# Mixture-of-experts stage: gate and up weights in one ring slot and one 512-column product per quadrant

## The chip, the cores and the metric

The kernel runs on one core of a Trainium2 chip. The metric is device time in microseconds (us); the kernel before takes 1612.64 us, the median of three runs (1609.98 to 1615.09).

## The reference, cut to what matters

Two layers of a hybrid attention network on 256 latent and 256 context tokens of width 1024, in float32. The last part, about half of the time, is the mixture of experts of layer 1: each of the 256 latent tokens goes to two of eight SwiGLU experts.

```python
for e in range(N_EXPERTS):          # 8 experts, D = 1024, FF = 2816
    out = out + combine[..., e:e + 1] * (silu(h @ wg[e]) * (h @ wu[e])) @ wd[e]
```

Every expert has three float32 matrices of 1024 x 2816; together they are 8 x 3 x 11.5 MB = 276.8 MB, and each byte is read from HBM once.

## The kernel before

**Tokens.** For each expert, `gather` (L966) picks the tokens that chose it into `gh`, up to 96 columns: three groups of 32. The third group holds tokens only where an expert was chosen by more than 64 of them. Products for the third group stand in a branch (`third`, L1011) that TensorE takes or skips by a register; the code of a skipped branch still lies in the program. In this input experts 1, 5, 6 and 7 take it, experts 0, 2, 3 and 4 skip it (experts are counted from 0).

**Columns.** FF is cut into three column groups `GR` (L910): 1024, 1024 and 768 columns. A product is cut over the four column quadrants of the array: `quads` (L1003) issues four products, each of 32 stationary columns and 256 (third group of columns: 192) moving columns, to PSUM partitions 0, 32, 64 and 96. I call these four products a set. Each product has 128 rows of the contraction behind it, one row block k; D has eight (KT = 8).

**One step** is one expert and one column group. `gate` (L1026) runs `half` (L1014): for each of eight row blocks, a set for token group 0 and one for group 1, then the branch with eight sets for group 2 into the bank `gu2`. Silu goes to ScalarE (L1034). `up` (L1037) does the same with the up matrix, into a second PSUM bank; the bank tag "mm" has two buffers. Between `gate` and `up` stand the transposes of the step before (`turn`), pieces of the output (`spread`), and the gathers of the next experts. After `up` comes `down` (L1073) of the step before: eight row blocks (six in the third column group), two sets each, and again a branch. So one step has three branches, and the eight experts have 72.

**Weights.** They pass through a ring of 14 slots of 8 KB per partition (1 MB; `ring`, L932 and L950). `load` (L935) fills one slot with one transfer of two row blocks of one matrix; `plan` (L921) lists them: four gate slots, four up slots, then four (three) down slots of the step before. `fetch` (L957) issues the load for a slot that comes free and hands out the oldest loaded one. All loads go through the queue of SyncE (SP), in order. A slot is free again once all its products are done, those in the branch too, so four slots are held until a branch is passed. The first four slots are loaded before the routing, while layer 1's mixer still runs.

After the last step come the last `turn`, `down`, `collect` and `spread`, and the output is stored.

Of the kernel before, what the change touches and what calls it, by code (L numbers as in the profile page):

```python
# [10 lines left out]
AF = mybir.ActivationFunctionType  # L11
# [4 lines left out]
D = 1024  # L16
KT = 8
# [5 lines left out]
NE = 8  # L23
# [3 lines left out]
LAT, CTX = (0, 1), (2, 3)  # L27
# [14 lines left out]
def build(tc, x, c, ctx, c_ctx, w_ada, b_ada, norm_mix, norm_ffn, w_in, w_out, a_q_gain, a_k_gain,  # L42
# [4 lines left out]
    dma = nc.sync.dma_start  # L47
    act, dve, pool, pe = nc.scalar, nc.vector, nc.gpsimd, nc.tensor
# [6 lines left out]
    def bank(tag, dt=F32):  # L55
        return psp.tile([128, 512], dt, name=tag, tag=tag, bufs=PB[tag])
# [24 lines left out]
    X = [Xl[:, 0], Xl[:, 1], Xc[:, 0], Xc[:, 1]]  # L81
# [28 lines left out]
    p = bank("tp")  # L110
# [4 lines left out]
    p = bank("tp")  # L115
# [44 lines left out]
    def krows(w, k0, kn, c0, cn):  # L160
        return w.rearrange("(k p) n -> p k n", p=128)[:, k0:k0 + kn, c0:c0 + cn]

    pin = tc.keep_in_program_order
# [739 lines left out]
    def moe(l):  # L903
# [6 lines left out]
        GR = ((0, 256), (1024, 256), (2048, 192))  # L910
        mark = [None, None, None]

        def up_rows(w, e, g):
            c0, n = GR[g]
            return [krows(w[m, e], 2 * j, 2, c0, 4 * n) for j in range(4)]

        def down_rows(wd, g):
            c0, n = GR[g]
            return [krows(wd, c0 // 128 + 2 * j, 2, 0, D) for j in range(n // 64)]

        def plan():  # L921
            prev = None
            for e in range(NE):
                for g in range(3):
                    for w in (moe_w_gate, moe_w_up):
                        yield from up_rows(w, e, g)
                    if prev:
                        yield from down_rows(moe_w_down[m, prev[0]], prev[1])
                    prev = e, g
            yield from down_rows(moe_w_down[m, prev[0]], prev[1])  # L930
# [1 line left out]
        ring = [(wa, f"wr{i}") for i in range(NRA)]  # L932
        count = [0]

        def load(src):  # L935
            p, t = ring[count[0] % len(ring)]
            count[0] += 1
            r = p.tile([128, 2048], F32, name="w", tag=t)
            a, b = src.shape[1:]
            v = r[:, 0:a * b].rearrange("p (a b) -> p a b", a=a)  # L940
            dma(v, src)
            return v

        todo = plan()
# [55 lines left out]
            act.copy(q, pt[0:CAP, 0:256].bitcast(F32))  # L1000
            return q

        def quads(ps, c0, lhsT, rhs, n, start, stop):  # L1003
            for q in range(4):
                o, r = ps[32 * q:32 * q + 32, c0:c0 + n], rhs[:, q * n:q * n + n]
                if n == 192:
                    o = o.rearrange("p (c i) -> p c i", c=3)
                    r = rhs.rearrange("p (c q i) -> p q c i", c=3, q=4)[:, q]
                pin(pe.matmul(o, lhsT, r, start=start, stop=stop, tile_position=(0, 32 * q), skip_group_check=True))  # L1009

        def third(m):  # L1011
            return tc.If(m > 0) if m is not None else ExitStack()

        def half(gh, n, pa, o, w, m):  # L1014
            vs = []
            for j in range(4):
                vs.append(w())
                for kk in range(2):
                    k = 2 * j + kk
                    for t in range(2):  # L1020
                        quads(pa, t * n, gh[:, k, 32 * t:32 * t + 32], vs[j][:, kk], n, k == 0 and t == 0, k == KT - 1)
            with third(m):
                for k in range(KT):
                    quads(gu2, o, gh[:, k, 64:96], vs[k // 2][:, k % 2], n, k == 0, k == KT - 1)

        def gate(gh, g, w, m=None):  # L1026
            n = GR[g][1]
            s = bank("mm"), bank("mm")
            sg = mp.tile([128, 832], F32, name="msg", tag="msg", bufs=2)
            if n == 192:  # L1030
                pool.memset(sg[:, 0:64], 0.0)
            s = *s, sg[:, 64:64 + 3 * n], sg
            half(gh, n, s[0], 0, w, m)
            act.activation(s[2][:, 0:2 * n], s[0][:, 0:2 * n], AF.Silu)  # L1034
            return s

        def up(gh, g, s, w, m=None):  # L1037
            n = GR[g][1]
            gA, uA, sg, full = s
            act.activation(sg[:, 2 * n:3 * n], gu2[:, 0:n], AF.Silu)  # L1040
            half(gh, n, uA, 256, w, m)
            dve.tensor_mul(sg[:, 0:2 * n], sg[:, 0:2 * n], uA[:, 0:2 * n])
            dve.tensor_mul(sg[:, 2 * n:3 * n], sg[:, 2 * n:3 * n], gu2[:, 256:256 + n])  # L1043
            return full

        def turn(sg, g):
            n = GR[g][1]
# [25 lines left out]
        def down(aT, g, py, w, m=None):  # L1073
            vs = []
            for i, ts in enumerate(aT):
                if i % 2 == 0:
                    vs.append(w())
                for t in range(2):
                    quads(py[0], 256 * t, ts[t], vs[-1][:, i % 2], 256, g == 0 and i == 0 and t == 0,
                          g == 2 and i == len(aT) - 1)  # L1080
            with third(m):
                for i, ts in enumerate(aT):
                    quads(py[1], 0, ts[2], vs[i // 2][:, i % 2], 256, g == 0 and i == 0, g == 2 and i == len(aT) - 1)

        def collect(py):
            ysb = mp.tile([CAP, D], F32, name="ysb", tag="ysb", bufs=1)
# [35 lines left out]
        def gathers(es_):  # L1122
            perm, gh = gather([col(posm, e) for e in es_], iota)
            for i, e in enumerate(es_):
                where[e] = perm, i, gh[:, i]
# [5 lines left out]
        more = [(big >> e) & 1 for e in range(NE)]  # L1131
        gathers((0, 1))
        units = []
        pend = None
        for e in range(NE):
            gh = where[e][2]
            for g in range(3):
                s = gate(gh, g, fetch, more[e])
                if pend:
                    aT = turn(pend[0], pend[1])  # L1140
                for _ in range(2):
                    if units:
                        spread(*units.pop(0))
                if g == 0:
                    py = [bank("at"), y2] if e == 0 else py
                if e % 2 == 1 and e < NE - 1 and g == 0:
                    gathers((e + 1, e + 2))
                if (e, g) == (NE - 2, 0):
                    gate_rows(l, 1, gm, (0,))
                if e == NE - 1 and g == 2:  # L1150
                    for t in LAT:
                        dve.tensor_mul(acc[:, t], acc[:, t], gm[:, 0])
                        dve.tensor_add(acc[:, t], acc[:, t], X[t])
                if g == 1:
                    qT = permT(where[e][0], where[e][1])
                sg = up(gh, g, s, fetch, more[e])
                if pend:
                    down(aT, pend[1], py, fetch, more[e - (pend[1] == 2)])
                    if pend[1] == 2:
                        ys = collect(py)  # L1160
                        units += [(qT, col(comb, e - 1), ys, t, dh, "tp", e == 1) for dh in range(2) for t in LAT]
                        py = [bank("at"), y2]
                pend = sg, g
# [7 lines left out]
        for rnd in range(1, (NL + CAP - 1) // CAP):  # L1171
            with tc.If(over > CAP * rnd):
                io = mp.tile([128, CAP], F32, name="io", tag="io")
                dve.tensor_scalar(io, iota, float(CAP * rnd), None, op0=OP.add)
                with tc.For_i(0, NE, 1) as e:
                    pc = mp.tile([128, 2, 2], F32, name="pc", tag="pc", bufs=1)
                    dve.tensor_copy(pc[:, :, 0:1], posm[:, :, bass.ds(e, 1)])
                    dve.tensor_copy(pc[:, :, 1:2], comb[:, :, bass.ds(e, 1)])
                    perm, gh = gather([[pc[:, t, 0:1] for t in LAT]] * 2, io)
                    qT = permT(perm, 0)  # L1180

                    def src(w):
                        return w[m, bass.ds(e, 1)].rearrange("o r n -> (o r) n")

                    def rows(parts):
                        it = iter(parts)
                        return lambda: load(next(it))

                    py = [bank("at"), y2]
                    for g in range(3):  # L1190
                        c0, n = GR[g]
                        ch = lambda w: [krows(src(w), 2 * j, 2, c0, 4 * n) for j in range(4)]
                        s = gate(gh[:, 0], g, rows(ch(moe_w_gate)))
                        sg = up(gh[:, 0], g, s, rows(ch(moe_w_up)))
                        down(turn(sg, g), g, py, rows(down_rows(src(moe_w_down), g)))
                    ys = collect(py)
                    for dh in range(2):
                        for t in LAT:
                            spread(qT, [pc[:, t, 1:2] for t in LAT], ys, t, dh, "tp", False, True)
# [120 lines left out]
```

## Time and profile before

| | |
|---|---|
| median of 3 runs | 1612.64 us |
| the profiled execution | 1617.77 us |
| its span, first to last instruction | 1616.0 us |
| TensorE busy over the span | 1508.8 us, 93% |
| weight loads busy (beside the products) | 1140.3 us, 71% |
| VectorE, ScalarE, GpSimd busy | 696.5, 482.3 and 2.9 us |
| mean transfer rate over the span | 245 GB/s |
| mean granted TensorE clock | 0.976 |

The profiled execution is 5.1 us above the median, and 1.8 us of it lie outside its span. Products are pipelined and their ends are modelled, so a busy TensorE need not be one at its peak. "issue" is idle time in which the engine waited for nothing that the profile shows. Instructions come through a transfer queue of their own, q8, in pieces of 16 KB; weights come through q1. Each semaphore step of a transfer is a packet under 512 B, 16 for each transfer.

### The profile page before, as it was taken

The numbers are of one execution on the slowest core, as the hardware profiler recorded it, in microseconds if no ns is written. First come the engines' busy times: TensorE is split into PE (matmuls) and PEld (weight loads), VectorE is DVE, ScalarE is ACT, GpSimd is POOL, SyncE is SP. The second block draws the span as 40 slices with busy tenths as digits, with TensorE's granted clock in tenths as the row PEclk, the third lists the DMA queues.
The fourth block names the chain that finished last, engine by engine and source line by source line (L and its number), as shares of the span: only waits on it lengthen the run. The fifth ranks groups of instructions, "written<-read, shape, count | busy, mean of one in ns | idle before, by whom it ended". The sixth has DMA issues, their size and how long they took to land. (4 is left out here: it accounts for less than half of the span.)

```text
span 1616.0 us, 38981 instructions
## 1 busy us (share of the span) xinstructions
PE 1508.8 (93%) x17126; PEld 1140.3 (71%) x17126; DVE 696.5 (43%) x1646; ACT 482.3 (30%) x1043; POOL 2.9 (0%) x17
## 2 busy tenths in 40 slices
PE   8999999999999999999997899998988899999996
PEld 6987767886998889788776566655564566656663
DVE  4797745797387744578954012020201011010122
ACT  3576663633223322267752011010201011110101
POOL 0000000000000000000000000000000000000000
PEclk9999999999999999999998999999999899999997
DMA  9443324265257733234328999999999998989970
GB/s 323 133 131 106 106 79 131 81 202 186 79 171 239 250 96 100 84 92 131 118 89 326 413 416 357 397 409 412 414 408 415 395 361 333 415 304 395 403 275 30
DMA packets 172148, 396.18 MB, mean 245 GB/s; under 512 B 10768, under 2 KB 89516, under 8 KB 171952
## 3 DMA queue, kind: packets, MB, share of 16 engines
q1 hardware_dynamic: 171952, 393.29, 65.9%
q8 instruction: 157, 2.57, 0.6%
q14 instruction: 39, 0.32, 0.1%
HBM read 392.21 MB, written 1.05 MB: 243 GB/s over the span
## 5 line engine op out<-in xcount | busy, mean ns | idle before, releaser
L1009 PE MATMUL mm<-w,gh 128*32 128x256 f32 (+1 forms) x6144 | 338.2, 367 | 27.1 <-issue 15.1
L1009 PEld LDWEIGHTS mm<-w,gh 128*32 128x32 f32 x6144 | 211.9, 111 | 138.3 <-issue 34.0
L1009 PE MATMUL at<-w,aT 128*32 128x256 f32 x3520 | 209.6, 387 | 13.4 <-issue 8.9
L148 ACT CAST w<-w 128x512 fp32r<-128x512 f32 (+1 forms) x244 | 138.5, 605 | 205.1 <-PE mm L167 87.2
L1009 PEld LDWEIGHTS at<-w,aT 128*32 128x32 f32 x3520 | 127.7, 112 | 89.3 <-issue 19.2
L153 DVE TENSOR_TENSOR w<-w 128x1024 fp32r<-128x1024 f32 (+1 forms) x122 | 144.8, 1186 | 98.8 <-ACT w L148 98.5
L1040 ACT ACTIVATE msg<-av 128x256 f32<-128x256 f32 (+1 forms) x24 | 8.8, 367 | 427.7 <-PE av L1009 239.4
L166 PE MATMUL mm<-w,hTh 128*128 128x256 f32 (+1 forms) x360 | 106.9, 298 | 3.2 <-ACT hTh L361 2.9
L167 PE MATMUL mm<-w,hTl 128*128 128x256 f32 (+1 forms) x360 | 106.7, 297 | 0.0
L168 PE MATMUL mm<-w,hTh 128*128 128x256 f32 (+1 forms) x360 | 106.4, 296 | 0.2 <-DVE w L153 0.2
L166 PE MATMUL mm<-w,aTh 128*128 128x256 f32 (+1 forms) x336 | 97.8, 291 | 0.0
L167 PE MATMUL mm<-w,aTl 128*128 128x256 f32 (+1 forms) x336 | 97.1, 289 | 0.0
L168 PE MATMUL mm<-w,aTh 128*128 128x256 f32 (+1 forms) x336 | 96.9, 289 | 0.0
L1054 DVE COPY aT<-tp 128x256 f32<-128x256 f32 x16 | 6.8, 425 | 182.5 <-PE tp L1053 182.5
L1009 PE MATMUL av<-w,gh 128*32 128x256 f32 (+1 forms) x1536 | 81.4, 361 | 0.0
L166 PEld LDWEIGHTS mm<-w,hTh 128*128 128x128 f32 x360 | 68.9, 192 | 7.8 <-ACT hTh L361 3.7
L167 PEld LDWEIGHTS mm<-w,hTl 128*128 128x128 f32 x360 | 69.0, 192 | 4.2 <-issue 2.0
L168 PEld LDWEIGHTS mm<-w,hTh 128*128 128x128 f32 x360 | 69.0, 192 | 4.0 <-issue 2.0
L166 PE MATMUL at<-hTh,w 128*128 128x512 f32 (+1 forms) x192 | 71.3, 373 | 0.3 <-ACT hTh L361 0.3
L167 PE MATMUL at<-hTh,w 128*128 128x512 f32 (+1 forms) x192 | 71.0, 371 | 0.0
L168 PE MATMUL at<-hTl,w 128*128 128x512 f32 (+1 forms) x192 | 70.9, 374 | 0.0
L1043 DVE TENSOR_TENSOR msg<-msg,av 128x256 f32<-128x256 f32 (+1 forms) x24 | 9.6, 398 | 140.7 <-PE av L1009 78.3
(373 smaller groups left out, 2556.0 us busy)
## 6 DMA issues: line engine op xcount, KB each, us to landing
w<-in_moe_w_down SPq DMA_DIRECT2D x88, 1024.0 KB, 10.6
w<-in_moe_w_gate SPq DMA_DIRECT2D x64, 1024.0 KB, 12.5
w<-in_moe_w_up SPq DMA_DIRECT2D x64, 1024.0 KB, 11.7
araw<-in_w_ada SPq DMA_DIRECT2D x80, 512.0 KB, 4.3
w<-in_moe_w_gate SPq DMA_DIRECT2D x32, 768.0 KB, 11.1
w<-in_moe_w_up SPq DMA_DIRECT2D x32, 768.0 KB, 7.8
w<-in_w_in SPq DMA_DIRECT2D x36, 512.0 KB, 3.7
w<-in_dense_w_gate SPq DMA_DIRECT2D x22, 512.0 KB, 5.0
```

The source lines that it names most:

```text
L148: act.copy(h[:, sl], r[:, sl])
L153: dve.tensor_sub(lo[:, sl], r[:, sl], h[:, sl].bitcast(F32))
L166: pe.matmul(ps, ah, bh, start=start, stop=False, skip_group_check=shared)
L167: pe.matmul(ps, al, bh, start=False, stop=False, skip_group_check=shared)
L168: return pe.matmul(ps, ah, bl, start=False, stop=stop, skip_group_check=shared)
L1009: pin(pe.matmul(o, lhsT, r, start=start, stop=stop, tile_position=(0, 32 * q), skip_group_check=True))
L1040: act.activation(sg[:, 2 * n:3 * n], gu2[:, 0:n], AF.Silu)
L1043: dve.tensor_mul(sg[:, 2 * n:3 * n], sg[:, 2 * n:3 * n], gu2[:, 256:256 + n])
L1054: (dve.tensor_copy if c0 else act.copy)(aT[:, c0:c1], pt[:, 0:c1 - c0])
```

## The change

The gate and the up rows of one row block share a ring slot: each slot is filled by two transfers of half a slot, one of either matrix. A product then takes both halves of the slot as its moving operand, 2 x 256 = 512 columns (2 x 192 = 384 in the third column group), and its result fills a PSUM bank with gate beside up. Token groups 0 and 1 have a bank each (the two "mm" buffers), group 2 has `gu2`. `gate` and `up` become `gate_up`: four row blocks for groups 0 and 1, a branch with four sets for group 2, the work that stood between `gate` and `up` (now handed in as `mid`), four more row blocks and a second branch. Then Silu and the multiply run once for each token group. The number of branches per step stays at three. `down`, its slots and its transfers stay as they were.

```diff
-        def up_rows(w, e, g):
+        def up_rows(wg, wu, g):
             c0, n = GR[g]
-            return [krows(w[m, e], 2 * j, 2, c0, 4 * n) for j in range(4)]
+            return [[krows(w, k, 1, c0, 4 * n) for w in (wg, wu)] for k in range(KT)]
...
-        def load(src):
+        def load(parts):
             p, t = ring[count[0] % len(ring)]
             count[0] += 1
             r = p.tile([128, 2048], F32, name="w", tag=t)
-            a, b = src.shape[1:]
-            v = r[:, 0:a * b].rearrange("p (a b) -> p a b", a=a)
-            dma(v, src)
+            v = r[:, 0:2 * parts[0].shape[2]].rearrange("p (a b) -> p a b", a=2)
+            n = 2 // len(parts)
+            for i, src in enumerate(parts):
+                dma(v[:, i * n:i * n + n], src)
             return v
...
+        def pairs(ps, lhsT, v, n, start, stop):
+            if n == 256:
+                o = lambda q: ps[32 * q:32 * q + 32].rearrange("p (u i) -> p u i", u=2)
+                r = lambda q: v[:, :, q * n:q * n + n]
+            else:
+                o = lambda q: ps[32 * q:32 * q + 32, 0:2 * n].rearrange("p (u c i) -> p u c i", u=2, c=3)
+                r = lambda q: v.rearrange("p u (c q i) -> p q u c i", c=3, q=4)[:, q]
+            quads(o, lhsT, r, start, stop)
...
+        def gate_up(gh, g, w, m, mid):
             n = GR[g][1]
-            s = bank("mm"), bank("mm")
+            ps = bank("mm"), bank("mm"), gu2
...
+            for k0 in (0, 4):
+                vs = [w() for _ in range(4)]
+                for k, v in enumerate(vs, k0):
+                    for t in range(2):
+                        pairs(ps[t], gh[:, k, 32 * t:32 * t + 32], v, n, k == 0, k == KT - 1)
+                with third(m):
+                    for k, v in enumerate(vs, k0):
+                        pairs(gu2, gh[:, k, 64:96], v, n, k == 0, k == KT - 1)
+                if k0 == 0:
+                    mid()
+            for t in range(3):
+                a = sg[:, 64 + t * n:64 + t * n + n]
+                act.activation(a, ps[t][:, 0:n], AF.Silu)
+                dve.tensor_mul(a, a, ps[t][:, n:2 * n])
+            return sg
```

## Rows read from the trace of the kernel before

**Rows 1.** The page: TensorE (busy tenths) and the transfer rate, 40 slices.
```profile
PE   8999999999999999999997899998988899999996
GB/s 323 133 131 106 106 79 131 81 202 186 79 171 239 250 96 100 84 92 131 118 89 326 413 416 357 397 409 412 414 408 415 395 361 333 415 304 395 403 275 30
```
**Rows 2.** Windows: each engine's busy us (instructions), granted clock, share of transfer engines, GB/s.
```profile
980.00:1000.00 20.00, 19.17 (x326) 12.99 (x318) 5.60 (x13) 4.61 (x10) 0.15 (x1) 1.00 0.98 392
1000.00:1020.00 20.00, 20.00 (x396) 12.67 (x392) 1.11 (x2) 0.00 (x0) 0.00 (x0) 1.00 0.81 298
1127.00:1212.00 85.00, 73.72 (x1196) 49.94 (x1192) 14.28 (x31) 10.71 (x24) 0.15 (x1) 0.98 1.02 411
1280.00:1301.00 21.00, 17.34 (x261) 10.90 (x264) 2.83 (x5) 0.20 (x1) 0.00 (x0) 0.83 1.00 390
1301.00:1597.00 296.00, 289.54 (x5282) 186.27 (x5274) 43.61 (x82) 30.86 (x71) 0.45 (x3) 1.00 0.84 329
```
**Rows 3.** Groups by line, 1301 to 1597: third-group products of the gate and up matrices.
```profile
L1009 PE MATMUL av<-w,gh 128*32 128x256 f32 (+1 forms) x1152 | 60.8, 361 | 0.0
```
**Rows 4.** Source L941 (the loads), issues of 1266 to 1273, with times to landing.
```profile
L941 SPq DMA_DIRECT2D w<-in_moe_w_gate x4: 368/394/421, 1266.1 to 1273.0; - x4
DMA to landing us min/median/max: 12.9/14.3/15.8
```
**Rows 5.** Timeline of TensorE from 1300: start, us, instructions; expert 5's first products.
```profile
1299.37 2.01 PE L1009 MATMUL at<-w,aT 128*32 128x256 f32 x16
1301.08 6.15 PE L1009 MATMUL mm<-w,gh 128*32 128x256 f32 x96
```
**Rows 6.** Waits of TensorE, 1045 to 1301: in total, times, longest.
```profile
PE mm L1009 <- issue: 11.5, 8, 3.0
PE mm L1009 <- PEq L1022: 7.0, 12, 2.7
PE mm L1009 <- DMA w<-in_moe_w_gate: 1.8, 2, 1.7
```
**Rows 7.** Timeline of TensorE, 1095 to 1102: a stall inside one run of products.
```profile
1094.72 2.02 PE L1009 MATMUL at<-w,aT 128*32 128x256 f32 x18
1099.46 1.71 PE L1009 MATMUL at<-w,aT 128*32 128x256 f32 x27 [2.73 <-issue]
```
**Rows 8.** Transfer queues: instruction pieces in 1097:1099, 1045:1301 and 1303:1587, in this order.
```profile
q8 instruction: 1, 0.02, 2.1%
q8 instruction: 41, 0.67, 1.0%
q8 instruction: 41, 0.67, 0.9%
```
**Rows 9.** Timeline of TensorE in expert 5, back to back: start, us, line, instructions.
```profile
1358.79 10.54 PE L1009 MATMUL at<-w,aT 128*32 128x256 f32 x192
1369.15 4.08 PE L1009 MATMUL mm<-w,gh 128*32 128x192 f32 x96
1373.05 2.78 PE L1009 MATMUL av<-w,gh 128*32 128x192 f32 x64
```
**Rows 10.** Windows with 768 KB (904, 1164) and with 1 MB transfers (920, 1182).
```profile
904.00:918.00 14.00, 12.41 (x182) 6.99 (x186) 1.51 (x3) 0.37 (x1) 0.15 (x1) 0.88 1.03 414
920.00:948.00 28.00, 22.74 (x410) 16.72 (x404) 1.33 (x3) 1.41 (x3) 0.00 (x0) 0.94 1.02 415
1164.00:1178.00 14.00, 12.99 (x204) 8.15 (x208) 3.65 (x9) 1.52 (x3) 0.15 (x1) 1.00 1.00 390
1182.00:1196.00 14.00, 9.56 (x178) 7.53 (x180) 1.83 (x3) 1.41 (x3) 0.00 (x0) 1.00 1.03 414
```
**Rows 11.** Source L203: issues of the 512 KB transfers of another stage, duration in ns.
```profile
L203 SPq DMA_DIRECT2D araw<-in_w_ada x48: 327/328/497, 240.4 to 561.5; - x48
```
**Rows 12.** Groups by line and form, 860 to 1616: Silu and multiply of the third group.
```profile
L1040 ACT ACTIVATE msg<-av 128x256 f32<-128x256 f32 x16 | 6.2, 384 | 235.2 <-PE av L1009 131.3 <-PEq L1022 103.9
L1043 DVE TENSOR_TENSOR msg<-msg,av 128x256 f32<-128x256 f32 x16 | 6.7, 421 | 103.5 <-PE av L1009 59.7 <-PEq L1022 43.8
```

More of the change, by code (lines that the diff above doesn't have):

```diff
@@ L911, in moe @@
         mark = [None, None, None]
-        def up_rows(w, e, g):
+        def up_rows(wg, wu, g):
             c0, n = GR[g]
-            return [krows(w[m, e], 2 * j, 2, c0, 4 * n) for j in range(4)]
+            return [[krows(w, k, 1, c0, 4 * n) for w in (wg, wu)] for k in range(KT)]
         def down_rows(wd, g):
             c0, n = GR[g]
-            return [krows(wd, c0 // 128 + 2 * j, 2, 0, D) for j in range(n // 64)]
+            return [[krows(wd, c0 // 128 + 2 * j, 2, 0, D)] for j in range(n // 64)]
         def plan():
@@ L924, in plan @@
                 for g in range(3):
-                    for w in (moe_w_gate, moe_w_up):
-                        yield from up_rows(w, e, g)
+                    yield from up_rows(moe_w_gate[m, e], moe_w_up[m, e], g)
                     if prev:
@@ L1001, in permT, with quads, rows256 @@
             return q
-        def quads(ps, c0, lhsT, rhs, n, start, stop):
+        def quads(ps, lhsT, rhs, start, stop):
             for q in range(4):
[L1005 to L1009, printed above, removed]
+                pin(pe.matmul(ps(q), lhsT, rhs(q), start=start, stop=stop, tile_position=(0, 32 * q), skip_group_check=True))
+        def pairs(ps, lhsT, v, n, start, stop):
[6 more added lines that the diff above has]
+            quads(o, lhsT, r, start, stop)
+        def rows256(ps, c0, lhsT, v, start, stop):
+            quads(lambda q: ps[32 * q:32 * q + 32, c0:c0 + 256], lhsT, lambda q: v[:, q * 256:q * 256 + 256], start, stop)
         def third(m):
             return tc.If(m > 0) if m is not None else ExitStack()
[L1014 to L1026, printed above, removed]
+        def gate_up(gh, g, w, m, mid):
             n = GR[g][1]
-            s = bank("mm"), bank("mm")
+            ps = bank("mm"), bank("mm"), gu2
             sg = mp.tile([128, 832], F32, name="msg", tag="msg", bufs=2)
@@ L1031, in gate @@
                 pool.memset(sg[:, 0:64], 0.0)
[L1032 to L1044, printed above, removed]
+            for k0 in (0, 4):
[13 more added lines that the diff above has]
+            return sg
         def turn(sg, g):
@@ L1078, in down @@
                 for t in range(2):
-                    quads(py[0], 256 * t, ts[t], vs[-1][:, i % 2], 256, g == 0 and i == 0 and t == 0,
-                          g == 2 and i == len(aT) - 1)
+                    rows256(py[0], 256 * t, ts[t], vs[-1][:, i % 2], g == 0 and i == 0 and t == 0,
+                            g == 2 and i == len(aT) - 1)
             with third(m):
                 for i, ts in enumerate(aT):
-                    quads(py[1], 0, ts[2], vs[i // 2][:, i % 2], 256, g == 0 and i == 0, g == 2 and i == len(aT) - 1)
+                    rows256(py[1], 0, ts[2], vs[i // 2][:, i % 2], g == 0 and i == 0, g == 2 and i == len(aT) - 1)
         def collect(py):
@@ L1133, in moe @@
         units = []
-        pend = None
+        pend = aT = py = qT = None
         for e in range(NE):
@@ L1137, in moe, with mid @@
             for g in range(3):
[L1138 to L1156, printed above, removed]
+                def mid(e=e, g=g):
+                    nonlocal aT, py, qT
+                    if pend:
+                        aT = turn(pend[0], pend[1])
+                    for _ in range(2):
+                        if units:
+                            spread(*units.pop(0))
+                    if g == 0:
+                        py = [bank("at"), y2] if e == 0 else py
+                    if e % 2 == 1 and e < NE - 1 and g == 0:
+                        gathers((e + 1, e + 2))
+                    if (e, g) == (NE - 2, 0):
+                        gate_rows(l, 1, gm, (0,))
+                    if e == NE - 1 and g == 2:
+                        for t in LAT:
+                            dve.tensor_mul(acc[:, t], acc[:, t], gm[:, 0])
+                            dve.tensor_add(acc[:, t], acc[:, t], X[t])
+                    if g == 1:
+                        qT = permT(where[e][0], where[e][1])
+                sg = gate_up(gh, g, fetch, more[e], mid)
                 if pend:
@@ L1190, in moe @@
                     for g in range(3):
[L1191 to L1194, printed above, removed]
+                        sg = gate_up(gh[:, 0], g, rows(up_rows(src(moe_w_gate), src(moe_w_up), g)), None, lambda: None)
                         down(turn(sg, g), g, py, rows(down_rows(src(moe_w_down), g)))
```

## The prediction

> **What bounds the kernel now.** The change touches the expert stage alone, so I read the page's slices first, to see where that stage lies: from about slice 22 (870 us) to the end TensorE is busy throughout and the transfer rate is near or at 415 GB/s [rows 1]. Both look full, so the next view is the windows, cut at the experts. They show two stretches [rows 2]. From 1301 to 1597, experts 5 to 7, TensorE is busy for 289.5 of 296 us at full clock and the transfers run at 329 GB/s: TensorE sets the pace. These are experts with a third token group (1152 records of its products, 384 for each of three experts) [rows 3]. Before 1301, with experts 2 to 4, transfers run at 411 GB/s with a share of 1.02, and TensorE is busy for only 73.7 of 85 us, at clock 0.98: there the transfers look like the limit, with TensorE waiting for weights.
>
> The third view says that it does not wait for weights. Expert 5's first gate slot is issued at 1266.1 and transfers of that time land 12.9 to 15.8 us after issue, median 14.3 [rows 4], so at about 1280.4; TensorE takes it up at 1301.1 [rows 5]. Weights lie ready for 20 us before use. And the idle time before 1301 is put down to "issue" (11.5 us for the "mm" products) and to the sequencer at the branch line (7.0), to gate transfers only 1.8 [rows 6].
>
> What then holds TensorE up? The fourth view, its timeline, has stalls inside a run of products, 2.73 us in one of them, where no branch and no new slot begins [rows 7]; one 16 KB piece of instructions arrives in just these microseconds [rows 8]. Pieces are counted: 41 from 1045 to 1301, one per 6.2 us. My estimate of the code from the source: a set is 16 instructions (four products, each with two weight loads and two records), a wide step 72 sets with its branches, 1152 instructions, a narrow one 66, 1056; an expert is 2 x 1152 + 1056 = 3360, and some 150 for transposes, gathers and spreads (2388 executed in 85 us [rows 2], less 140 sets or 2240). 3510 x 3 / 41 = 257 instructions per piece, so the code of skipped branches is fetched too. Experts 5 to 7 take 41 pieces as well, over 284 us [rows 8]. So before 1301 TensorE is fed instructions at one piece per 6.2 us while transfers are saturated: 13.7 pieces or 85 us per expert, though the executed sets need 108 x 0.432 + 32 x 0.325 = 57 us [rows 9], some 62 with transposes and gathers (my estimate). It happens that 85 us is also nearly what the transfers need: 34.6 MB at 414 GB/s [rows 10] are 83.6 us. Hence a full ring beside full transfers.
>
> A rule of the Trainium skill, "Runtime: NRT & Kernel Launch", section "Instruction fetch mechanics", says that pieces of 256 instructions are fetched ahead, sequentially and mostly hidden, and that a taken branch with its target outside the fetched window stalls. The first half fits 256 and not "hidden" (2.73 us in mid-run); by the second half alone the stalls would stay, since the branches stay at 72. That is rival B.
>
> **The change, part by part.**
>
> *Products.* Back to back, 24 sets of 256 columns take 1358.79 to 1369.15, 431.7 ns each; 12 of 192 take 1369.15 to 1373.05, 325.0 [rows 9]. That is 1.667 ns per column and 5 ns fixed. A set of 512 replaces two of 256: 858.5 against 863.4 ns. The same columns pass; only the 5 ns go, 480 times in the stage, 216 times after 1301: 1.1 us. No row shows quadrants with 512 columns; the bounds are 0 and 2 us gain, since 192 to 256 is linear. I take 1.
>
> *Instructions.* The gate and up sets halve: a wide step has 2 x (128 + 64) + 384 = 768 instructions, a narrow one 672, an expert 2208 + 150 = 2358, 9.2 pieces, at 6.2 us 57 us. For experts 0, 2, 3, 4 this falls below their products (62) and the transfers (84). TensorE then runs ahead until the ring is empty, and what is late next is the weights. While it was two near-equal limits, one is left, the transfers; expert 5 starts when its first slot lands and no longer 20.7 us later (1301.1 - 1280.4). This is the term that carries the forecast.
>
> *Transfers recovered.* During expert 1 (third group, TensorE slow) the ring was full and transfers idled: 392 and 298 GB/s in two windows of 20 us [rows 2], against 414: 20 x (1 - 392/414) + 20 x (1 - 298/414) = 6.7 us. With the ring nearly empty when expert 1 starts, there is room, and all later landings come up to 6.7 us earlier. I take 6.
>
> *Half transfers.* 116 more transfers pass before expert 5 (24 slots for each of five experts, less four loaded earlier). SP issues one in 0.33 us [rows 11], two per 2.5 us of slot transfer, so its queue is not the limit; "free slot" is waited for once per slot as before, and down's loads stand behind it as before. For a fixed cost per transfer I compare 768 KB with 1 MB: 414 against 415 GB/s with a deep queue (1.900 and 2.527 us; a line through both has 0.02 us at zero bytes), 390 against 414 at 1164 (2.016 and 2.533; 0.465 us) [rows 10]. So 2 to 54 us, never a gain. I take 2: after the change the queue is deep, as in the first pair, and in the second the ring was full and SP waited for slots.
>
> *Expert 5 from an empty ring.* Its first four slots land 2.5 us apart, 7.5 us in all, and the last slot's products follow (two sets, 1.7 us): 9.2 instead of 6.9. Loss 2.3, and after that its products are slower than the transfers. *Clock.* After stalls the clock falls to half; the window before expert 5 has 0.83 over 21 us, 3.6 us lost [rows 2]. Waits for weights could do the same: 0 to 4, I take 2.
>
> *One PSUM bank per token group.* The next step's first product now waits for Silu and multiply of the same bank, 384 and 421 ns [rows 12], three pairs in a row about 1.7 us. `down`'s 7.8 us or more on TensorE hides it. Only between the first and second step there is no `down`; about 1 us once, absorbed by expert 0's surplus. ScalarE and VectorE do one instruction more per step; both are nearly idle. Branches, `mid` and `down` have the same place in the order; two semaphores per slot instead of one on TensorE's sequencer run ahead of the products: 0.
>
> Sum: 20.7 + 6 + 1 - 2 - 2.3 - 2 = 21.4 us. The profiled execution, 1617.8 with 1.8 outside its span, comes to 1596.4; taken from the median, 1612.6 - 21.4 = 1591.
>
> **The rivals.**
>
> *A, smaller (the lead is only partly released).* Expert 0 to 4 still stall on some pieces: in `down`, 384 instructions per 7 us of executed products exceed one piece per 6.2 us, and the clock falls there. If half of the 20.7 us stays, 1601. For it: `down` is not made denser. Against: on average over a step there is slack of 84 to 57.
>
> *B, no change.* The stalls belong to taken branches, 72 as before, and each costs the same: expert 5 starts where it did, 1 us of column gain, 1611. For it: 7.0 us stand at the branch line [rows 6]. Against: the stall in mid-run [rows 7] and pieces in proportion to all code [rows 8].
>
> *C, slower.* Half transfers have a fixed cost that shows when the ring is always waiting for them. At 0.465 us it is 54 us up to expert 5: 1591 + 52 = 1643. It decides from (21.4 + 2) / 116 = 0.20 us per transfer. For it: the second pair of [rows 10]. Against: the first pair, and the share of 1.02 at 411 GB/s, which leaves no idle time between transfers of 1 MB. The Trainium skill, "DMA: Bandwidth & Descriptors", section "Anatomy of one DMA — SWDGE (gpsimd) path", gives a fit of about 2 us per transfer plus bytes at 436 GB/s; were that not overlapped, 116 x 2 = 232 us would be added. The rows disagree at 1 MB, 2.53 us a transfer and not 4.4.
>
> **How the numbers follow.** A measurement can tell 0.3%, 4.8 us, from no change. Forecast 0.66, 1591, its own range 1580 to 1600; A 0.13, 1601; B 0.13, 1611; C 0.08, up to 1643. The range reaches down to 1579 (no clock loss, no first-slot loss, full recovery, and 5 us for the spread of the median) and up to 1607, which takes in A and leaves out B and C, 0.21. Faster: forecast and A, 0.79; same: B, 0.13; slower: C, 0.08.
>
> **What would show it.** Instruction pieces per skipping expert fall from 13.7 to about 9; TensorE's waits before expert 5 change from "issue" to transfers; expert 5 starts near 1280 and lasts with 6 and 7 for about 295 us still; weights lie ready for a few us at most before expert 5. Wrong it is if TensorE's waits stay "issue" at the same cadence (B), if the rate before expert 5 falls under 400 GB/s (C), or if products of 512 columns take over 870 ns a set.

## The result and the profile after

The kernel after takes 1585.74 us (median of four runs, 1584.25 to 1589.97), the one before 1611.31 in the four runs beside them: 0.9851 of the time, interval 0.9829 to 0.9872, so 25.6 us or 1.5% less. The forecast was 1591 us with a range of 1579 to 1607. The profiled execution of after took 1584.25 us, its span is 1582.5 us. The medians leave out one slow run, 1698.70 us at a mean granted clock of 0.84, the fourth run of the changed kernel with another order of experts.

First the slices of the page, as in [rows 1]: the granted clock, in tenths, and the rate.

```profile
PEclk9999999999999999999998999999999999999997
GB/s 322 144 133 108 108 67 134 69 200 224 69 169 213 261 135 87 107 64 132 126 41 280 415 416 415 415 416 403 417 407 416 405 416 406 417 373 399 399 242 30
```

From slice 23 to 35 the rate stays between 403 and 417 GB/s, where [rows 1] have dips to 357, 361 and 333. The clock has its one dip in slice 22, ahead of the experts, and then holds until the last slice.

Next the windows as in [rows 2], with the same columns: expert 1, experts 3 and 4, and experts 5 to 7 of after.

```profile
930.00:1026.00 96.00, 94.07 (x1131) 45.39 (x1127) 14.84 (x34) 11.23 (x27) 0.15 (x1) 1.00 1.03 416
1096.00:1180.00 84.00, 72.17 (x809) 31.21 (x802) 14.84 (x34) 11.23 (x27) 0.15 (x1) 1.00 1.02 412
1180.00:1265.00 85.00, 69.92 (x775) 26.91 (x770) 12.22 (x26) 9.19 (x23) 0.15 (x1) 1.00 1.02 411
1265.00:1561.00 296.00, 288.03 (x3550) 128.01 (x3550) 45.02 (x92) 32.43 (x80) 0.45 (x3) 1.00 0.90 356
```

Expert 3 takes 84 us in after and 85 in [rows 2], with nearly the same busy time of TensorE (72.2 and 73.7 us) and the same rate. By that view alone nothing has changed. What TensorE waits for has changed. Its waits from 1026 to 1265 (experts 2 to 4; in total, times, longest), beside [rows 6]:

```profile
PE mm L1005 <- DMA w<-in_moe_w_up: 11.5, 22, 0.8
PE at L1005 <- DMA w<-in_moe_w_down: 8.8, 15, 1.5
PE mm L1005 <- PEq L1033: 2.7, 8, 0.4
```

The 11.5 us of "issue" are gone, the branch line went from 7.0 to 2.7 us, and 20.3 us in short waits for transfers have come. Instruction pieces of the same stretch, as in [rows 8]:

```profile
q8 instruction: 27, 0.44, 0.7%
```

That is 27 pieces for three experts, 9.0 each, and not 13.7. Expert 5 starts at its first landed slot (timeline of TensorE, as [rows 5]; in brackets the idle time before and what ended it):

```profile
1259.89 1.93 PE L1005 MATMUL at<-w,aT 128*32 128x256 f32 x32 [0.61 <-DMA w<-in_moe_w_down]
1262.74 1.93 PE L1005 MATMUL at<-w,aT 128*32 128x256 f32 x32 [0.92 <-PEq L1079]
1265.01 1.92 PE L1005 MATMUL mm<-w,gh 128*32 128x512 f32 x16 [0.33 <-DMA w<-in_moe_w_up]
1268.02 1.92 PE L1005 MATMUL mm<-w,gh 128*32 128x512 f32 x16 [1.08 <-DMA w<-in_moe_w_up]
1270.31 1.92 PE L1005 MATMUL mm<-w,gh 128*32 128x512 f32 x16 [0.37 <-DMA w<-in_moe_w_up]
```

Where the time went. The stage of the experts begins with the first gather product, and so do the two timelines below, before first, then after:

```profile
869.93 0.50 PE L982 MATMUL tp<-perm,xnh 128*128 128x192 f32 x1 [2.31 <-DVE perm L972]
```

```profile
863.87 0.50 PE L982 MATMUL tp<-perm,xnh 128*128 128x192 f32 x1 [2.31 <-DVE perm L972]
```

The 6.1 us between them lie ahead of the change, in code that is the same in both; the kernels run below, none of which touches that code either, begin their stage between 865 and 868 us, so this is a spread from run to run, and I count from the stage's start:

| us | before | after | gain |
|---|---|---|---|
| stage start to expert 5 | 431.2 (1301.1 - 869.9) | 401.1 (1265.0 - 863.9) | 30.1 |
| experts 5 to 7, to the last product of a weight | 295.8 (to 1596.9) | 295.9 (to 1560.9) | -0.1 |
| from there to the end of the span | 19.1 | 21.6 | -2.5 |
| the stage | 746.1 | 718.6 | 27.5 |

Everything was gained before expert 5. The stage's 27.5 us stand beside 25.6 us between the medians.

### The profile page after: what moved, and what is told of

Read it like the earlier page. It is cut to its first block, busy times and chain, and to the rows that moved or that the text cites. A ratio compares the mean times of both kernels' runs of the same rounds, so it can differ in the third digit from the quotient of the medians.

```text
span 1582.5 us, 31693 instructions
## 1 busy us (share of the span) xinstructions
PE 1486.6 (94%) x13286; PEld 994.2 (63%) x13286; DVE 700.1 (44%) x1670; ACT 486.1 (31%) x1067; POOL 2.9 (0%) x17
## 5 line engine op out<-in xcount | busy, mean ns | idle before, releaser
L1005 PE MATMUL mm<-w,gh 128*32 128x512 f32 (+1 forms) x3072 | 327.5, 559 | 18.0 <-DMA w<-in_moe_w_up 13.3
L1005 PEld LDWEIGHTS mm<-w,gh 128*32 128x32 f32 x3072 | 102.8, 110 | 210.8 <-issue 185.1
L1005 PE MATMUL at<-w,aT 128*32 128x256 f32 x3520 | 202.4, 380 | 12.7 <-DMA w<-in_moe_w_down 8.8
L1005 PEld LDWEIGHTS at<-w,aT 128*32 128x32 f32 x3520 | 118.9, 110 | 100.3 <-DMA w<-in_moe_w_down 19.4
L1005 PE MATMUL av<-w,gh 128*32 128x512 f32 (+1 forms) x768 | 81.1, 557 | 0.0
L1068 DVE COPY aT<-tp 64x256 f32<-64x256 f32 x8 | 3.4, 428 | 149.1 <-ACT aT L1066 149.1
```

The source lines that it names most:

```text
L1005: pin(pe.matmul(ps(q), lhsT, rhs(q), start=start, stop=stop, tile_position=(0, 32 * q), skip_group_check=True))
L1068: (dve.tensor_copy, act.copy)[i % 2](at[64:128, 4 * i:hi], pv[64:128, 0:hi - 4 * i, :, 1])
```

## The experiments

My theory: skipping experts (0, 2, 3, 4) are held by the supply of instructions, one piece of 16 KB in about 6.2 us, code of skipped branches included; the change matters because it halves the gate and up instructions. Rival B: the cost sits in the branches that are taken past the code, however long that code is. Two more rivals: the gain is in the shape of the products, and the half transfers cost something that a gain elsewhere hides. The kernel before took 1612.45 us beside the first four kernels (up to the branch body four times) and 1610.98 beside the other three.

**The same products in two halves.** After, but every product of 512 columns is issued as two of 256, into the same bank. Slots, transfers, banks, branches and order are those of after; only the instructions are as many as before.

```diff
-            quads(o, lhsT, r, start, stop)
+            for u in range(2):
...
+                    o = lambda q: ps[32 * q:32 * q + 32, u * n:u * n + n]
+                    r = lambda q: v[:, u, q * n:q * n + n]
...
+                quads(o, lhsT, r, start and u == 0, stop)
```

> The changed kernel, but each product of 512 columns is issued as two of 256, gate and then up, into the same bank; slots, half transfers, order, branches and banks stay as changed. This puts the instructions of a skipping expert back from about 2360 to about 3510. Theory (TensorE is fed instructions at one piece of 256 per 6.2 us while transfers are saturated): stalls put down to issue come back before expert 5 and the time goes back to 1605 to 1616 us. Rival (the gain comes from the shared slot, the shorter branches or the bank per token group): it stays at 1582 to 1590.

Measured: 1612.12 us, 0.9995 of before (0.9978 to 1.0012). The whole gain is gone. Pieces and waits of TensorE in experts 2 to 4 (1043 to 1295):

```profile
q8 instruction: 41, 0.67, 1.0%
```

```profile
PE mm L1005 <- issue: 12.7, 7, 3.0
PE mm L1005 <- PEq L1034: 8.5, 13, 2.4
```

41 pieces in 252 us are 6.15 us each, and the waits are again those of [rows 6]. So the gain hangs on the number of instructions, and the shared slot, the half transfers, the banks and the new place of the branches come to nothing together.

**Less skipped code in before.** Before, but in experts 0, 2, 3 and 4 the branches that are never taken hold half their sets. What TensorE executes there, the number of branches and the transfers are unchanged; what is left out is code that does not run.

```diff
+LEAN = 0, 2, 3, 4
...
-                for k in range(KT):
+                for k in range(1, KT, 2) if lean else range(KT):
...
-                for i, ts in enumerate(aT):
+                for i, ts in list(enumerate(aT))[1::2] if lean else enumerate(aT):
```

> The kernel before, and in the four experts whose branch is skipped the branch bodies hold half their sets (one for each ring slot, so that slots are held as long). Nothing that is executed here changes; the branches stay at 72. An expert's code falls from 3510 to about 2950 instructions, 11.5 pieces, 71 us at 6.2 us each, under the 84 us of its transfers. Theory: the ring runs empty before expert 5 and nearly the whole gain of the change comes without it, 1584 to 1594 us. Rival (taken branches) and rival (column or weight-load savings): no change, 1607 to 1615.

Measured: 1589.6 us, 0.986 of before (0.9824 to 0.9895). Removing code that is never executed brings nearly all that the change brings. Pieces, waits and the window of experts 2 to 4 (1030 to 1271):

```profile
q8 instruction: 35, 0.57, 0.9%
```

```profile
PE mm L1010 <- DMA w<-in_moe_w_gate: 11.7, 20, 1.9
PE at L1010 <- DMA w<-in_moe_w_down: 9.4, 16, 1.0
PE mm L1010 <- PEq L1023: 1.6, 9, 0.2
```

```profile
1030.00:1271.00 241.00, 208.70 (x3540) 126.73 (x3528) 37.79 (x77) 27.99 (x64) 0.46 (x3) 1.00 1.02 413
```

11.7 pieces per expert, waits for transfers, full clock, 413 GB/s: the picture of after, with products of 256 columns and as many branches taken as before. The wait at the branch line falls from 7.0 [rows 6] to 1.6 us: those waits were for code, too.

**Half transfers alone.** The kernel of the last paragraph, and each gate or up slot is filled by two transfers of half the size.

```diff
-            dma(v, src)
+            for i in range(a if split else 1):
+                dma(v[:, i:i + 1] if split else v, src[:, i:i + 1] if split else src)
```

> As e3_less_dead, and each gate and up slot is filled by two half transfers, one per row block, instead of one. It measures the fixed cost of a transfer where the ring runs empty. Theory (0.02 us each, 116 more of them before expert 5): 0 to 4 us over e3_less_dead. Rival C (0.2 to 0.465 us each): 23 to 54 us over it.

Measured: 1586.6 us, 0.9848 of before (0.9817 to 0.9879), 3.0 us under the kernel with whole transfers; their runs overlap (1584.4 to 1588.8 against 1584.7 to 1592.5), so there is no cost, and a gain is not shown. The window of experts 2 to 4:

```profile
1028.00:1269.00 241.00, 212.53 (x3548) 125.27 (x3544) 37.80 (x77) 27.98 (x64) 0.45 (x3) 1.00 1.02 410
```

The same 241 us and 410 GB/s against 413.

**More skipped code in after, twice.** After, but in the skipping experts the body of `gate_up`'s branch stands four times in the program, in a second kernel eight times. The copies never run; nothing else is changed.

```diff
-                    for k, v in enumerate(vs, k0):
-                        pairs(gu2, gh[:, k, 64:96], v, n, k == 0, k == KT - 1)
+                    for _ in range(4 if idle else 1):
+                        for k, v in enumerate(vs, k0):
+                            pairs(gu2, gh[:, k, 64:96], v, n, k == 0, k == KT - 1)
...
+                sg = gate_up(gh, g, fetch, more[e], mid, e in (0, 2, 3, 4))
```

> The changed kernel, and in the four experts whose branch is skipped the branch bodies of gate and up stand four times in the program. Nothing more is executed; only never-executed code grows, until an expert's code is 3510 instructions again. Theory (skipped code is fetched too, and the pieces set the pace): 1605 to 1616 us, with some 13.7 pieces per skipping expert. Rival (fewer products and weight loads on TensorE are what gained): 1582 to 1590. Rival (each taken branch stalls by itself): 1582 to 1590, since there are 72 as before.

Measured: 1628.38 us, 1.0112 of before (1.0075 to 1.0149). The gain is gone, as the theory has it, but the time is 12 us above the upper end that I had expected. Pieces and waits of experts 2 to 4 (1045 to 1309):

```profile
q8 instruction: 41, 0.67, 0.9%
```

```profile
PE mm L1005 <- PEq L1033: 20.3, 12, 4.6
PE mm L1005 <- DMA w<-in_moe_w_up: 12.5, 4, 4.1
```

As many pieces as before, 41, but in 264 us, 6.4 us each; the longest wait at the branch line is 4.6 us, where [rows 6] have 2.7. The time of a piece is thus no constant, and I let the second kernel ask whether saturated transfers are what stretches it.

> As e2_dead_code, with the bodies of gate and up standing eight times in the skipping experts: about 5050 instructions or 19.7 pieces an expert. Theory with one piece per 6.2 us whatever the transfers do: 122 us for each of the four skipping experts and 1740 to 1770 us. Theory with pieces that come faster once transfers leave room: the pace is then set by both together, some 95 to 105 us an expert, 1640 to 1700. Rival (skipped code costs nothing): 1582 to 1590.

Measured: 1693.95 us, 1.0515 of before (1.0492 to 1.0537). Pieces, waits and the window of experts 2 to 4:

```profile
q8 instruction: 58, 0.95, 1.2%
```

```profile
PE mm L1005 <- PEq L1033: 28.9, 8, 5.5
PE mm L1005 <- DMA w<-in_moe_w_up: 17.1, 4, 5.2
PE mm L1005 <- DMA w<-in_moe_w_gate: 13.0, 3, 4.9
PE mm L1005 <- issue: 11.9, 2, 7.4
```

```profile
1057.00:1376.00 319.00, 235.81 (x2385) 105.74 (x2380) 39.38 (x86) 29.60 (x73) 0.46 (x3) 0.86 0.87 328
```

TensorE executes what it does in after (2385 products against 2384 from 1026 to 1265) and needs 319 us in place of 239. The 58 pieces are 19.3 per expert. By the source an expert now has 2358 + 7 x 384 = 5046 instructions, 19.7 pieces, so the whole of the skipped code is fetched. Transfers have idle time now, 328 GB/s at a share of 0.87, and still TensorE waits: 319 / 58 = 5.5 us a piece on average. So the supply is a limit of its own and not only a victim of full transfers; beside full ones a piece took 6.2 us [rows 8], which is longer by an eighth. An expert that skips its third group takes 106 us here, one that computes it (expert 1) 95.5 us.

The 30.1 us put down to transfers in these rows show no lack of weights. By the semaphores of the trace all seven of these waits end 0.19 us behind the branch line's event, as do the eight put down to that line; the transfer named is one of which a packet landed last. (With the body four times, 9.8 of the 16.6 us put down to gate and up transfers are of this kind; for the two other waits, 6.8 us, the trace does not settle it.) It is SyncE that waits: it cannot issue the next loads until TensorE has passed a branch and so freed the slots (waits of SyncE, 1057 to 1376).

```profile
SPq L941 <- PEq L1033: 136.0, 17, 9.9
```

**Another order of the experts.** In after, the experts that compute a third group are slower than the transfers (about 96 us against 84), and those that skip it are faster, if the transfers let them. They stand in a row at the end. The next two kernels take the experts in the order 0, 1, 5, 2, 6, 3, 7, 4, once in after and once in before. The order suits this input.

```diff
+ORD = 0, 1, 5, 2, 6, 3, 7, 4
...
-                    yield from up_rows(moe_w_gate[m, e], moe_w_up[m, e], g)
+                    yield from up_rows(moe_w_gate[m, ORD[e]], moe_w_up[m, ORD[e]], g)
...
-        more = [(big >> e) & 1 for e in range(NE)]
+        more = [(big >> e) & 1 for e in ORD]
...
```

> The changed kernel with the experts in the order 0, 1, 5, 2, 6, 3, 7, 4, so that experts that take the third group stand between experts that skip it and the last one skips. Theory (skipping experts are limited by transfers, 84 us each, the others by TensorE, about 97 us, and the ring of some 25 us evens them out): transfers run without a pause and end near 1512 in the span instead of 1535, little stays to do after them, and the time is 1535 to 1560 us. Rival (the ring doesn't even them out, each expert costs the longer of its two times): as the change, 1582 to 1590.

Measured, order in after: 1562.78 us (median of three runs, 1559.48 to 1564.75), 0.9696 of before (0.9673 to 0.9719). It beats both kernels, by 48 and 23 us, and is 3 us above the end of what I had expected. Its last weights land at 1529.5, 9 us before the last product, where I had reckoned with 1512. Windows of expert 6 (with a third group), 3 (without), and the last, 4:

```profile
1199.00:1289.00 90.00, 88.52 (x1085) 40.76 (x1081) 12.22 (x26) 9.19 (x23) 0.15 (x1) 1.00 1.03 416
1289.00:1365.00 76.00, 72.06 (x868) 36.15 (x860) 14.13 (x30) 11.23 (x27) 0.15 (x1) 1.00 1.02 410
1459.00:1539.00 80.00, 75.59 (x934) 36.19 (x926) 18.67 (x36) 10.85 (x28) 0.15 (x1) 1.00 0.88 353
```

A pair of one expert with and one without a third group now takes 166 us, about what its transfers need (2 x 83.6 us, as the prediction works out), and both TensorE and the transfers are near full in either window.

> The kernel before with the same order of experts. Theory (instructions hold its skipping experts at 85 us while transfers are saturated, so TensorE never catches up in them): 4 x 97 + 4 x 85 us as in the old order, 1600 to 1618 us. Rival (the skipping experts were limited by transfers and only the order cost time): 1545 to 1575.

Measured, order in before: 1598.3 us, 0.9915 of before (0.9899 to 0.9932), 12.7 us gained in place of the 23 that the order gains in after, and 2 us under the range I had expected. Its last expert, 4 (1491 to 1581):

```profile
1491.00:1581.00 90.00, 80.44 (x1302) 50.13 (x1294) 18.29 (x32) 10.33 (x25) 0.15 (x1) 0.94 0.75 302
```

Its waits in the same window:

```profile
PE mm L1010 <- issue: 4.0, 4, 2.7
PE mm L1010 <- PEq L1023: 2.2, 5, 1.5
```

It needs 90 us at 302 GB/s, with idle transfers, against 80 in the window above, and the waits are for instructions: with those of before a skipping expert cannot run at the pace of its products even where weights are there.

## Why the prediction was right

**The bound.** That instructions and not weights held experts 2 to 4 was read from a stall in mid-run and from counted pieces [rows 7, 8]. (The view of 1097:1099 has `q8 instruction: 1, 0.02, 3.3%`; the first line of [rows 8] is that of 1197:1200. It is one piece in either.) Less skipped code in before and the split products in after show it from both sides: each changes the number of instructions and little or nothing else, and each moves the time by about the whole effect (22.9 and 26.4 us against 25.6). Rival B falls with the first of them, whose branches are taken as often as before. The Trainium skill, "Runtime: NRT & Kernel Launch", section "Instruction fetch mechanics", calls the fetch of sequential pieces mostly hidden; here the traces disagree, since removing skipped code brought 23 us.

**The lead, +20.7, and the recovery, +6.** Together they came to about what was forecast and more: expert 5 starts 30.1 us earlier in the stage, where the terms up to there (20.7 + 6 - 2 - 2) gave 22.7. The lead is released wholly: no weights lie ready at 1265.01 in the timeline above, so rival A falls. The remaining 9.4 us are an earlier landing (410.5 us from the stage's start in before, 1280.4 - 869.9, and 401.1 in after). For its greater part it is the recovery, which I had from two windows of 20 us. The whole of expert 1 in before, and experts 2 to 4:

```profile
949.00:1045.00 96.00, 94.08 (x1708) 63.69 (x1703) 14.38 (x31) 10.72 (x24) 0.15 (x1) 1.00 0.97 383
1045.00:1301.00 256.00, 219.81 (x3548) 142.09 (x3544) 37.88 (x77) 28.04 (x64) 0.45 (x3) 0.96 1.02 409
```

Against 416 GB/s in the same expert of after that is 96 x (1 - 383/416) = 7.6 us, and 256 x (1 - 409/411) = 1.2 us more behind it: 8.8 of the 9.4. The rest is within the 12.9 to 15.8 us of the landing times from which I took the median [rows 4].

**Half transfers, -2.** They cost nothing that shows: 411 GB/s before expert 5 in after, 410 with and 413 without them in the pair of experiments, and rival C, which needed 0.20 us each, falls. The lower end of the bounds, from the pair with a deep queue [rows 10], was the right one. The Trainium skill's fit of about 2 us per transfer plus bytes ("DMA: Bandwidth & Descriptors", section "Anatomy of one DMA — SWDGE (gpsimd) path") did not show here either: twice as many gate and up transfers passed in the same 241 us. That page gives it for transfers of the gpsimd path; these are issued by SyncE, several of them under way at a time.

**Clock, -2.** It was not lost. In after the granted clock is 1.00 in every window above, where [rows 2] have 0.83 ahead of expert 5. The waits for transfers are 22 of at most 0.8 us and 15 of at most 1.5 us, spread over the stretch, the earlier ones up to 3.0 us long [rows 6]; in the kernel with the branch body eight times the waits are up to 7.4 us and the clock is 0.86.

**Expert 5 from an empty ring, -2.3.** The waits of its first slots add up to 0.33 + 1.08 + 0.37 = 1.8 us. **Products, +1.** Runs of products in expert 5 (start, us; four, six, four and two sets):

```profile
1304.43 4.02 PE L1005 MATMUL av<-w,gh 128*32 128x512 f32 x32
1313.28 5.36 PE L1005 MATMUL mm<-w,gh 128*32 128x512 f32 x48
1318.45 3.62 PE L1005 MATMUL av<-w,gh 128*32 128x512 f32 x32
1321.88 1.90 PE L1005 MATMUL mm<-w,gh 128*32 128x512 f32 x16
```

From 1318.45 to 1321.88 four sets take 3.43 us, 857.5 ns each; from 1313.28 to 1318.45 six take 861.7 each; forecast were 858.5. Together these two terms leave experts 5 to 7 at 295.9 us against 295.8; the third-group products of [rows 3] stay at the same busy time:

```profile
L1005 PE MATMUL av<-w,gh 128*32 128x512 f32 (+1 forms) x576 | 60.4, 557 | 0.0
```

**One PSUM bank per token group, 0.** In experts 2 to 4 one product waits for the multiply, 0.9 us and in `down` at that; the "mm" products wait for transfers and the branch line alone, and in experts 5 to 7 for transfers alone, 1.8 us in all. `down` is shorter than the prediction has it in an expert that skips its third group, 12 sets or 5.2 us at the least and not 7.8, but that still hides the 1.7 us.

**Not foreseen: the end, -2.5.** From the last product of a weight to the end of the span after takes 21.6 us and before 19.1. The engines do the same work there: the last VectorE instruction ends at 1606.8 in before, 9.8 us behind that product, and at 1570.4 in after, 9.5 us behind it. What is longer is the rest, 9.2 and 12.1 us, in which the output lands and the program ends. The three kernels made from before and profiled with it took 17.7 to 19.6 us for the whole, those made from after 21.1 to 22.2, and with the split products it is 21.2, so the number of products is not what does it.

The traces show where the time goes: SyncE waits at the line of the branches that follow the last expert. These branches hold rounds for experts with more than 96 tokens and are skipped here; in after their code, too, has two transfers for each gate or up slot. Waits of SyncE (1606:1616 in before, 1569:1583 in after) and pieces of another instruction queue, q14 (1607:1616 and 1570.5:1582.5), before first, then after:

```profile
SPq L1172 <- SPq L1172: 6.4, 4, 3.0
q14 instruction: 4, 0.03, 1.0%
SPq L1171 <- SPq L1171: 9.2, 4, 2.9
q14 instruction: 6, 0.05, 1.3%
```

These 2.8 us are nearly all of the 2.9 between 9.2 and 12.1. The three kernels made from before wait 4.7 to 6.9 us there, those made from after 8.5 to 9.8; the shortest wait is that of the kernel with half transfers, which has them in the experts and not in the skipped rounds. So it is most likely skipped code once more, this time SyncE's; no kernel changed it alone.

Summed up for the profiled executions: 21.4 us were forecast; the losses to transfers and clock did not happen (+4), the recovery was mis-sized, 8.8 for 6 (+2.8), the landing was 0.6 us earlier than estimated, first slots and products together cost 0.1 in place of 1.3 us (+1.2), and the end took 2.5 back: 27.5, with 25.6 between the medians. That the total came so near to 21.4 owes something to chance, as the end took back part of what the other terms were too small by. And the range was added up wrongly: the terms named for its lower end make 10.0 us, which gives 1581 and not 1579; the measured time lies above either.

**What stays open.** Why a piece takes 6.4 us with the branch body four times, 6.2 in before and 5.5 with it eight times. Full transfers alone don't explain it, since the first has a lower rate than before (394 GB/s against 409). It may be that pieces can be fetched ahead only so far, so that code in large lumps, between long runs of products, uses the time badly; no kernel here tried lumps of another size with the same amount of code. The packets of the traces show that the mean hides much: in before the pieces of experts 2 to 4 come 5.5 to 10.0 us apart, with the branch body eight times 0.1 to 11.6 us. One view of the latter, 1275:1276:

```profile
q8 instruction: 2, 0.03, 23.8%
```

## What to carry to other kernels

Where an engine stalls inside a run of like instructions with "issue" as the reason, count the instruction pieces of the stretch against the time, and count the code of the branches that are not taken among them: a branch spares the execution, not the fetch. A change that lets one instruction do the work of two can then be worth more than its own nanoseconds, but only in stages where the engine has less to execute than to fetch; here that was 30.1 us in the first five experts and nothing in the last three. Two limits that happen to be equal (85 us of instructions, 84 of transfers) look like one in a table of windows; the timeline of the waiting engine tells which it is, and once one is gone, work that is slower and faster than the other can be interleaved for a second gain (23 us).

## What the runs showed of the hardware

- Code that is never executed takes time on TensorE's path: 2688 more skipped instructions in each of four experts cost 108 us (1693.95 against 1585.74), that is 10.1 ns for each of the 10752.
- Where TensorE waits for its code, a 16 KB piece of instructions came every 5.5 us on average with transfers at 328 GB/s (58 in 319 us), and every 6.2 us beside full transfers (41 in 256 us). This is no floor: with the branch body eight times single pieces came 0.1 us apart.
- Gate and up transfers of 512 and 384 KB, with 1 MB ones for down, move 410 to 411 GB/s back to back, where the slots filled by one transfer each gave 409 and 413.
- The products with three token groups run at the pace of their columns at 256 and 512 alike: 431.7 ns for a set of 256 [rows 9] and 857.5 to 861.7 ns for one of 512.
